# Keys and values of a memory: computed in the opening of the program, with their weights loaded in turn with those of a modulation

## The chip, the cores and the metric

One NeuronCore of a Trainium2 chip runs the whole program. The metric is the time of one execution on the device, in microseconds (us); shown is the median of repeated runs. PE is TensorE, DVE is VectorE, ACT is ScalarE, POOL is GpSimd, and SP is the queue that issues most DMA loads.

## What is computed

Two models stand one after the other. The first has two hybrid layers over 512 latent and 256 context tokens of width 1024. Each layer normalizes and modulates the tokens, with shift, scale and gate from silu(c) @ w_mod, multiplies by w_in (3584 columns), and mixes by a short convolution, an attention, a gated scan (hgrn) and a Fourier mix, then multiplies by w_out. The second model has one layer: a window attention and a gated delta rule side by side, a cross attention to a memory of 256 rows, and a swiglu. What the change moves is the memory's part of that cross attention; in the reference's terms:

```
m  = rms_norm(mem, g_mem)              # 256 x 1024
kv = m @ w_ckv                         # 1024 x 2048: 1024 columns of keys, 1024 of values
```

It depends on nothing of the first model. The first modulation, on which all of layer 0 depends, is

```
shift, scale, gate = split(silu(c) @ w_mod + b_mod, 3)    # w_mod: 1024 x 3072 per layer
```

## The kernel before, in words

Every large product runs in float32 precision as three matmuls (`mm3`, lines 189 to 191): each operand is split into a high part (an ACT copy, line 194) and a low part (a subtraction, line 195, on DVE or, where `pool_lo` is set, on POOL). Weights come in units of 1 MB (`wraw`, line 279, two buffers `raw`), are split into tiles `wh` and `wl` of 128 x 512 (four buffers of each, which is one unit), and the split of the next unit follows PE through those buffers, one unit ahead. A unit of 256 columns against 256 columns of tokens is 48 matmuls of 128 x 256.

The program builds instructions in the order of the Python code, by generators that several places advance in turn, and a scheduler then orders each engine's queue; what stands in a queue runs in that order.

**Start** (`start`, `mod_first`, lines 330 to 362, and `start_ctx`). The context rows are loaded, scaled by their root mean square (`rowscale`, lines 416 to 418) and transposed (line 532). The shift and scale columns of w_mod for layer 0 come in eight tiles `mraw` of 1 MB, one for each k, and four matmuls `modA` for each accumulate the modulation in PSUM (line 346). Then the first weight unit of layer 0 and the rows of x are loaded. At the end modA is copied, transposed (line 318) and made into A and B (`mod_ab`), the context is rescaled with them (line 512, tile `xc`) and split, and the first layer matmuls (`gc` for context columns, `gl` for latent ones) begin. The gate rows of the modulation come later, in steps between the layers' matmuls; the first of these matmuls is line 380.

**The memory** (`memkv`, lines 673 to 720) is a generator of nine steps. The first loads and scales the 256 rows and transposes them into `mch` and `mcl`, high and low part (lines 428, 445, 446). Four steps make the keys, two groups of 24 matmuls each, and four the values, likewise. A result leaves PSUM by an ACT copy into a tile `t` of two buffers (lines 705, 718) and goes to DRAM by a DMA on ACT's queue (lines 706, 719). Its units of w_ckv are split one ahead.

It runs in three places. The first step stands in the attention of layer 1 (line 1042). The keys follow that attention in `layer` (lines 560 to 563); in PE's queue they fill the attention's last part. The values are made at the beginning of `part2` (lines 1184 to 1190), that is, after the output projection of layer 1 (`out_proj`, tile `wo`), whose last rows are meanwhile normalized and transposed (`to_xT`) for part 2.

**Attention of layer 1.** For a token tile and a head PE makes scores (lines 1058, 1059), DVE the maximum (line 1063), ACT the exponential (line 1066), DVE the scaling (line 1068), PE six transposes (line 1074), ACT and DVE copy them, and PE multiplies with the values (line 1083).

**Part 2** begins in `mix` with a product for values, alpha and beta (144 columns, token tiles 0 to 3 in turn, lines 1306 to 1318), then a group of 128 columns (`dn_proj`). Beside them run `rope2`, which loads the positions by ACT's queue (line 1440) and makes sines on DVE and ACT (lines 1443 to 1460), and `dn_gates`, a chain of small DVE operations from alpha to the gates, whose first matmul is line 1566.

Of the kernel before, what the change touches and what calls it, by code (L numbers as in the profile page):

```python
# [9 lines left out]
F32 = mybir.dt.float32  # L10
# [12 lines left out]
T = S + CTX  # L23
# [4 lines left out]
def constants():  # L28
# [54 lines left out]
    # window masks [query, key]: block before (key >= query), block after (key <= query)  # L83
# [6 lines left out]
class Cols:  # L90
    """a [128, T] operand in two tiles: latent columns and context columns"""
# [9 lines left out]
def pair(t, pr):  # L101
    """the columns of two token tiles of t [128, 512]"""
    if pr[1] == pr[0] + 1:
        return t[:, 128 * pr[0]:128 * pr[0] + 256]
    return t[:, 0:S].rearrange("p (a c) -> p a c", c=128)[:, pr[0]:pr[1] + 1:pr[1] - pr[0]]


class Ahead:
    """split weight units in the order of their use, one ahead"""
# [14 lines left out]
class PhasePool:  # L124
    """sets K.ps_s for a phase"""
# [12 lines left out]
class Slots:  # L138
    """tiles in given places, by tag"""
# [8 lines left out]
class K:  # L148
    order = ((0, 1), (2, 3))
    # rows of w_out in the order in which they get ready: hgrn, fourier, conv, attention  # L150
# [46 lines left out]
    def load_early(self):  # L197
        """identity, parameters as columns, silu of the conditions"""
# [10 lines left out]
        # silu(c), silu(c_ctx) as 32 column operands, two used  # L209
# [5 lines left out]
    def lower_bounds(self):  # L215
        nc, cst = self.nc, self.cst
        # hgrn lower bounds: logits in col 32..39 as (d, l, j)
# [9 lines left out]
        # per (d, j): bias lb + floor, scale 1 - lb  # L227
# [8 lines left out]
    def load_late(self, tp):  # L236
        """constants of part 2"""
# [17 lines left out]
        # a_log, dt_bias, sink on every partition  # L255
# [3 lines left out]
    def rpow(self, out, ss, scale, eps, n):  # L259
        """out = (ss * scale + eps) ** -0.5 on small [128, n]"""  # L260
# [5 lines left out]
    def wraw(self, srcs, kk, cols):  # L266
        """raw tile [128, kk, cols]; srcs: list of (col0, dram ap [kk*128, n])"""
# [14 lines left out]
    def wsplit(self, raw_view, tiles=None):  # L282
        """[128, kk, ...] -> list of (hi, lo) [128, cols] over k, at most 512 columns in a tile; tiles: others than the usual"""
# [21 lines left out]
    def mod_rows(self, t, l, c0, n):  # L305
        """bias rows of w_mod columns c0.. in t [32 n + stream, 512], the rest zero"""
# [6 lines left out]
    def mod_ab(self, l, mr):  # L313
        """A = g (1 + scale), B = shift as [128, stream, 8] of mr rows (shift 0, 1, scale 0, 1)"""
# [15 lines left out]
    def mod_first(self, mp, side):  # L330
        """shift and scale of layer 0"""
# [3 lines left out]
        next(side)  # L335
        def load(k):
            raw = mp.tile([128, 2048], F32, tag="mraw", name="mraw", bufs=5)
            nc.sync.dma_start(raw, self.I["w_mod"][0, 128 * k:128 * k + 128, 0:2048])
            return raw

        raws = [load(k) for k in range(5)]
        for k in range(8):
            raw = raws[k]
            next(side, None)
            for n in range(4):
                nc.tensor.matmul(pa[32 * n:32 * n + 32], self.cact[:, k, :], raw[:, 512 * n:512 * n + 512],
                                 start=(k == 0), stop=(k == 7))
            if k < 3:
                raws.append(load(k + 5))
            if k == 2:  # L350
                self.pool_lo = True
                self.first = self.hgrn_w(self.I["w_in"][0], 0)
                self.pool_lo = False
                self.xrows = []
                for i in range(4):
                    h = mp.tile([128, 1024], F32, tag="h", name="h", bufs=6)
                    nc.sync.dma_start(h, self.I["x"][0, 128 * i:128 * i + 128, :])
                    self.xrows.append(h)
        for _ in side:
            pass  # L360
# [3 lines left out]
    def mod_rest(self):  # L364
        """gate rows of both layers to DRAM, shift and scale of layer 1: a step per MB of weights"""
# [3 lines left out]
        def gates(l):  # L369
            # rows 64 q + 32 n + stream: columns 512 n of the k tiles of parity q  # L370
# [40 lines left out]
    def rowscale(self, h, pool):  # L411
        """h [128, 1024] -> h / rms(h) rows, in place"""
# [8 lines left out]
    def to_xT(self, xs, pr, xh, xl, A, B, pool):  # L421
        """xs: row-scaled token tiles of the pair pr; their columns of xh/xl[k]"""
# [25 lines left out]
    def lat_gemm(self, us, tags):  # L448
        """psum [128 ch, 512] per unit; first all units on the first 256 tokens"""
# [1613 lines left out]
```

## Time and profile before

| | |
|---|---|
| median of 3 runs | 1797.39 us |
| lowest, highest | 1796.39, 1798.08 us |
| span of the profiled execution | 1802.5 us |
| busy: PE, PE weight loads, DVE, ACT, POOL | 94%, 75%, 56%, 50%, 13% of the span |
| mean granted TensorE clock | 0.974 |
| DMA, all loads and stores | 193.79 MB, mean 108 GB/s |

The profile gives the span of one execution, the time from its first to its last instruction; the timed runs are others, so both are named. Busy shares are means over stages with different limits. Matmuls overlap, so a PE that is busy all the time may still follow its operands; the distance between the starts of two matmuls says more than their lengths.

### The profile page before, as it was taken

What the parts mean: (1) busy time and instruction counts of PE and PEld (TensorE: products, weight loads), DVE (VectorE), ACT (ScalarE), POOL (GpSimd) and SP (SyncE); (2) the same over time, 40 slices, a digit from 0 to 9 for tenths busy, and PEclk for the clock granted to TensorE, in tenths of its full rate; (3) what the DMA queues carried; (4) which work ended last, traced back from release to release, by engine and by line L of the source; (5) the groups of instructions that cost most, each with busy time, mean ns of one, the idle gap of its engine ahead of it and who ended that gap; (6) DMA issues with size and microseconds to landing.
All of it is one profiled execution on the core that took longest, in us unless ns stands there. A gap on an engine that the chain in (4) does not pass through costs nothing.

```text
span 1802.5 us, 30443 instructions
## 1 busy us (share of the span) xinstructions
PE 1693.4 (94%) x12155; PEld 1357.9 (75%) x12155; DVE 1017.6 (56%) x2127; ACT 902.7 (50%) x1850; POOL 232.4 (13%) x250
## 2 busy tenths in 40 slices
PE   6999889999989988999999888999999999999998
PEld 3876767878768665877878667877788788888886
DVE  4446373565474646476576898568766733333233
ACT  4756562442458765353565833465655633333222
POOL 2100001101131000100022434002000111111000
PEclk8999999999999999999999998899999999999999
DMA  8231203200454211301764233110743723332531
GB/s 351 106 115 49 94 25 133 88 1 26 147 183 143 95 48 38 111 24 53 251 213 143 87 90 94 42 48 1 215 136 107 248 79 94 94 94 84 174 105 70
DMA packets 162570, 193.79 MB, mean 108 GB/s; under 512 B 15054, under 2 KB 124910, under 8 KB 160252
## 3 DMA queue, kind: packets, MB, share of 16 engines
q1 hardware_dynamic: 156604, 183.37, 31.3%
q10 hardware_dynamic: 5824, 8.47, 1.6%
q8 instruction: 95, 1.56, 0.4%
q14 instruction: 47, 0.39, 0.1%
HBM read 175.28 MB, written 13.66 MB: 105 GB/s over the span
## 4 chain that ended last, share of the span: by engine, by line
PE 69%; DVE 13%; ACT 8%; issue 4%; DMA 2%; POOL 2%; ACTq 0%; SPq 0%; POOLq 0%; DVEq 0%
PE mm L189 7%; PE mm L190 7%; PE mm L191 7%; PE gl L189 4%; PE gl L190 4%; PE gl L191 4%; DVE acc L1603 2%; PE tr L1083 2%; DVE wl L195 2%; PE sc L1059 1%; PE tr L1074 1%; PE sc L946 1%; ACT S L860 1%; PE tp L189 1%; PE tp L190 1%
## 5 line engine op out<-in xcount | busy, mean ns | idle before, releaser
L194 ACT ACTIVATE wh<-raw 128x512 fp32r<-128x512 f32 (+1 forms) x458 | 282.6, 628 | 409.0 <-PE mm L190 161.0
L195 DVE TENSOR_TENSOR wl<-raw,wh 128x512 fp32r<-128x512 f32 x416 | 285.1, 699 | 358.2 <-ACT wh L194 350.4
L189 PE MATMUL mm<-xh,wh 128*128 128x512 f32 x520 | 208.3, 401 | 1.4 <-ACT acc L1601 1.0
L190 PE MATMUL mm<-xl,wh 128*128 128x512 f32 x520 | 208.3, 401 | 0.0
L191 PE MATMUL mm<-xh,wl 128*128 128x512 f32 x520 | 208.1, 401 | 0.0
L189 PE MATMUL gl<-xh,wh 128*128 128x512 f32 (+1 forms) x480 | 181.3, 378 | 1.3 <-ACT lf L754 0.6
L191 PE MATMUL gl<-xh,wl 128*128 128x512 f32 (+1 forms) x480 | 180.1, 376 | 0.3 <-DVE wl L195 0.3
L190 PE MATMUL gl<-xl,wh 128*128 128x512 f32 (+1 forms) x480 | 179.7, 375 | 0.1
L189 PEld LDWEIGHTS mm<-xh,wh 128*128 128x128 f32 x520 | 100.6, 193 | 23.2 <-ACT acc L1601 1.9
L191 PEld LDWEIGHTS mm<-xh,wl 128*128 128x128 f32 x520 | 100.3, 193 | 20.4
L190 PEld LDWEIGHTS mm<-xl,wh 128*128 128x128 f32 x520 | 100.3, 193 | 20.2 <-issue 0.3
L189 PEld LDWEIGHTS gl<-xh,wh 128*128 128x128 f32 x480 | 91.7, 191 | 23.0 <-issue 6.0
L191 PEld LDWEIGHTS gl<-xh,wl 128*128 128x128 f32 x480 | 91.7, 191 | 19.0 <-issue 4.9
L190 PEld LDWEIGHTS gl<-xl,wh 128*128 128x128 f32 x480 | 91.8, 191 | 15.5 <-issue 2.8
L195 POOL TENSOR_TENSOR wl<-raw,wh 128x512 fp32r<-128x512 f32 x42 | 59.6, 1425 | 108.0 <-ACT wh L194 73.5
L189 PE MATMUL gc<-ch,wh 128*128 128x256 f32 x224 | 65.7, 295 | 4.1 <-ACT ch L194 2.7
L190 PE MATMUL wo<-wl,yh 128*128 128x512 f32 x160 | 65.1, 408 | 4.2 <-DVE wl L195 4.2
L190 PE MATMUL gc<-cl,wh 128*128 128x256 f32 x224 | 65.2, 291 | 1.8 <-DVE cl L195 1.8
L191 PE MATMUL gc<-ch,wl 128*128 128x256 f32 x224 | 65.1, 291 | 0.0
L191 PE MATMUL wo<-wh,yl 128*128 128x512 f32 x160 | 63.6, 399 | 0.0
L189 PE MATMUL wo<-wh,yh 128*128 128x512 f32 x160 | 63.4, 402 | 0.0
L1979 POOL TENSOR_TENSOR al<-t,ah 128x512 fp32r<-128x512 f32 x22 | 28.3, 1286 | 211.6 <-ACT ah L1978 211.6
(596 smaller groups left out, 3926.4 us busy)
## 6 DMA issues: line engine op xcount, KB each, us to landing
raw<-in_w_in SPq DMA_DIRECT2D x32, 1024.0 KB, 4.9
raw<-in_w_gate_up SPq DMA_DIRECT2D x44, 512.0 KB, 4.8
raw<-in_w_mod SPq DMA_DIRECT2D x16, 1024.0 KB, 6.3
raw<-in_w_out SPq DMA_DIRECT2D x12, 1024.0 KB, 5.3
raw<-in_w_down SPq DMA_DIRECT2D x10, 1024.0 KB, 4.9
mraw<-in_w_mod SPq DMA_DIRECT2D x8, 1024.0 KB, 12.0
raw<-in_w_out SPq DMA_DIRECT2D x16, 512.0 KB, 6.5
raw<-in_w_ckv SPq DMA_DIRECT2D x8, 1024.0 KB, 5.0
```

The costliest lines, as they stand in the source:

```text
L189: mm(out, ah, bh, start=start, stop=False)
L190: mm(out, ah, bl, start=False, stop=False)
L191: mm(out, al, bh, start=False, stop=stop)
L194: self.nc.scalar.activation(hi, src, AF.Copy)
L195: (eng or self.nc.vector).tensor_tensor(lo, src, hi.bitcast(F32), ALU.subtract)
L860: nc.scalar.activation(so.rearrange("p v c -> p c v"), up, AF.Copy)
L946: nc.tensor.matmul(o[32 * A:32 * A + 32, p, 64 * i:64 * i + 64], *t[n_], start=(n_ == 0), stop=(n_ == len(t) - 1))
L1059: nc.tensor.matmul(s_[:, c0:c0 + n], qi[hs], kl[hs, ks], start=False, stop=True)
L1074: nc.tensor.transpose(tr[:, 128 * ii:128 * ii + 128], P[:, 128 * (t0 + ii):128 * (t0 + ii) + 128], self.ident)
L1083: nc.tensor.matmul(o[64 * h:64 * h + 64], kv[:, k0 + kt, 128 + 64 * h:192 + 64 * h], PTs[h][:, 128 * kt:128 * kt + 128], start=(kt == 0), ...
L1603: nc.vector.scalar_tensor_tensor(acc, pad[:, t:t + 512], cw, acc, ALU.mult, ALU.add)
L1979: nc.gpsimd.tensor_tensor(al[j], t, ah[j].bitcast(F32), ALU.subtract)
```

## The change

`mod_first` now begins with the memory. It makes the generator `memkv`, takes its first step, and then takes one step of it for each of the eight k of w_mod: a unit of keys or values, then a load of a later w_mod tile, then a step of the context's transposes (from k = 2 on), then the four modA matmuls of k. Two w_mod tiles are asked for ahead of the loop, with four buffers in place of five. The first weight unit of layer 0 is loaded and split after the loop, its low parts no longer on POOL, and the rows of x are asked for at k = 6. `memkv` loads its first weight unit before it scales the rows, and uses tiles of the start's pool. The three old places are gone. (The edit also drops comments and docstrings, which changes line numbers: a line here can be 1 to 4 off from the old one.)

```diff
     def mod_first(self, mp, side):
         pa = self.psum("sm", [128, 512], "modA")
         mr = mp.tile([128, 512], F32, tag="mr", name="mr")
-        next(side)
         def load(k):
-            raw = mp.tile([128, 2048], F32, tag="mraw", name="mraw", bufs=5)
+            raw = mp.tile([128, 2048], F32, tag="mraw", name="mraw", bufs=4)
             nc.sync.dma_start(raw, self.I["w_mod"][0, 128 * k:128 * k + 128, 0:2048])
             return raw
-        raws = [load(k) for k in range(5)]
+        self.mkp = mp
+        mem = self.memkv(mp)
+        next(mem)
+        raws = [load(k) for k in range(2)]
+        self.xrows = []
         for k in range(8):
-            raw = raws[k]
-            next(side, None)
+            next(mem)
+            if k < 6:
+                raws.append(load(k + 2))
+            if k >= 2:
+                next(side, None)
             for n in range(4):
-                nc.tensor.matmul(pa[32 * n:32 * n + 32], self.cact[:, k, :], raw[:, 512 * n:512 * n + 512],
+                nc.tensor.matmul(pa[32 * n:32 * n + 32], self.cact[:, k, :], raws[k][:, 512 * n:512 * n + 512],
                                  start=(k == 0), stop=(k == 7))
-            if k < 3:
-                raws.append(load(k + 5))
-            if k == 2:
-                self.pool_lo = True
-                self.first = self.hgrn_w(self.I["w_in"][0], 0)
-                self.pool_lo = False
-                self.xrows = []
+            if k == 6:
                 for i in range(4):
                     h = mp.tile([128, 1024], F32, tag="h", name="h", bufs=6)
                     nc.sync.dma_start(h, self.I["x"][0, 128 * i:128 * i + 128, :])
                     self.xrows.append(h)
+        for _ in mem:
+            pass
+        self.first = self.hgrn_w(self.I["w_in"][0], 0)
         for _ in side:
             pass
...
     def layer(self, l):
-                if l:
-                    self.mkp = ap
-                    for _ in range(4):
-                        next(self.mem)
...
     def memkv(self, mk):
         for i in range(2):
-            h = mk.tile([128, 1024], F32, tag="mem", name="mem", bufs=2)
+            h = mk.tile([128, 1024], F32, tag="h", name="mem", bufs=6)
             nc.sync.dma_start(h, I["mem_2"][0, 128 * i:128 * i + 128, :])
+            xs.append(h)
+        w = I["w_ckv_2"][0]
+        units = Ahead(...)
+        units.more()
+        for h in xs:
...
         self.to_xT(xs, (0, 1), mh, ml, self.col[:, c0:c0 + 8], None, mk)
         yield
-        w = I["w_ckv_2"][0]
-        units = Ahead(...)
...
     def attention(self, l, w_in, need, ap):
-        if l:
-            self.mem = self.memkv(ap)
-            next(self.mem)
...
     def part2(self):
-            self.mkp = mk
-            for _ in self.mem:
-                pass
```

SP's queue at the very beginning of the program; `mem` is the memory, `mraw` w_mod, `h` context or x, `raw` a weight unit. Before:

```order
L524 DMA h<-in_ctx 128x1024 x2
L338 DMA mraw<-in_w_mod 128x2048 x8
L279 DMA raw<-in_w_in 128x8x128 x2
L357 DMA h<-in_x 128x1024 x4
L497 DMA k_blockones<-in_c_blockones 128x128
```

and with the change:

```order
L681 DMA mem<-in_mem 128x1024 x2
L279 DMA raw<-in_w_ckv 128x8x256
L337 DMA mraw<-in_w_mod 128x2048 x2
...
L528 DMA h<-in_ctx 128x1024 x2
L337 DMA mraw<-in_w_mod 128x2048
L279 DMA raw<-in_w_ckv 128x8x256 x2
...
L358 DMA h<-in_x 128x1024 x4
L279 DMA raw<-in_w_in 128x8x128 x2
L501 DMA k_blockones<-in_c_blockones 128x128
```

The eight w_mod tiles stood together behind the context; now the memory stands first, units of w_ckv and tiles of w_mod take turns, the context comes after five of them, and x and the first unit of w_in after all.

PE's queue at the end of the attention of layer 1; `sc` are scores, `tr<-early,P` transposes, `tr<-PT,kv` products with the values, `mm<-mch,wh` the memory's keys, `wo` the output projection. Before:

```order
L1074 MATMUL tr<-early,P 128x128 x6
L189 MATMUL mm<-mch,wh 128x256
L190 MATMUL mm<-mcl,wh 128x256
L191 MATMUL mm<-mch,wl 128x256
...
L1083 MATMUL tr<-PT,kv 64x128 x12
L189 MATMUL mm<-mch,wh 128x256
...
L191 MATMUL mm<-mch,wl 128x256
L189 MATMUL wo<-wh,yh 128x512
```

and with the change:

```order
L1073 MATMUL tr<-early,P 128x128 x6
L1057 MATMUL sc<-kh,qs 128x512
L1058 MATMUL sc<-kl,qs 128x512
L1057 MATMUL sc<-kh,qs 128x256
L1058 MATMUL sc<-kl,qs 128x256
L1073 MATMUL tr<-early,P 128x128 x6
L1082 MATMUL tr<-PT,kv 64x128 x12
L1073 MATMUL tr<-early,P 128x128 x12
L1082 MATMUL tr<-PT,kv 64x128 x12
L189 MATMUL wo<-wh,yh 128x512
```

Before, 57 of the memory's matmuls stood between these rows and 135 between the last product with the values and the projection's first matmul; now 18 matmuls of the projection stand ahead of the last two heads' scores, and its 19th comes right behind the last product.

ACT's queue where part 2 begins; `xh` are high parts of the transposed rows, `pos` the positions, `rp` the sines, `V` the evacuation of part 2's first product, `vd<-t` the store of memory values, `wh` split weights. Before:

```order
L445 ACTIVATE xh<-tr,col 128x256 x2
L719 DMA vd<-t 128x256
L1562 ACTIVATE al<-bc 128x8
L1440 DMA pos<-in_positions 128x1024
L718 ACTIVATE t<-mm 128x256
...
L1456 ACT_TABLE_LOAD
L1456 ACTIVATE rp_10221<-ra,k_invf 128x512
L1460 ACTIVATE rp_10221<-ra 128x512
L1317 ACTIVATE V<-mm 128x128 x3
L194 ACTIVATE wh<-raw 128x512 x4
```

and with the change:

```order
L449 ACTIVATE xh<-tr,col 128x256 x8
L1313 ACTIVATE V<-mm 128x128
L1558 ACTIVATE al<-bc 128x8
L1436 DMA pos<-in_positions 128x1024
L1313 ACTIVATE V<-mm 128x128 x2
L194 ACTIVATE wh<-raw 128x512
L1452 ACT_TABLE_LOAD
L1452 ACTIVATE rp_10221<-ra,k_invf 128x512
L194 ACTIVATE wh<-raw 128x512 x3
L1313 ACTIVATE V<-mm 128x128
```

Before, the sines were made ahead of the first evacuation `V`, while the memory's values ran; now the positions' load stands behind the first of them, and the sines between the third and the fourth, ahead of three weight splits.

## Rows read from the trace of the kernel before

**Rows 1.** The page, costliest groups: engine, operation, tiles, count, busy us, mean ns.

```profile
L195 DVE TENSOR_TENSOR wl<-raw,wh 128x512 fp32r<-128x512 f32 x416 | 285.1, 699 | 358.2 <-ACT wh L194 350.4
```

**Rows 2.** Busy us of each engine by stretch, then granted clock, DMA share, GB/s.

```profile
0.00:10.00 10.00, 1.76 (x3) 0.37 (x3) 2.40 (x15) 5.07 (x8) 1.54 (x7) 1.00 0.82 316
...
10.00:20.00 10.00, 9.16 (x53) 3.01 (x54) 2.82 (x7) 1.53 (x4) 0.55 (x1) 1.00 1.01 425
...
30.00:40.00 10.00, 5.54 (x25) 5.24 (x26) 9.24 (x21) 6.19 (x14) 6.03 (x7) 0.51 1.05 407
```

**Rows 3.** Timeline of PE in the start: start us, length, operation, count, idle before.

```profile
10.53 0.47 PE L532 MATMUL mm<-early,h 128*128 128x128 f32 x1
...
12.25 1.93 PE L346 MATMUL modA<-mraw,cact 128*32 128x512 f32 x6
...
16.77 0.38 PE L532 MATMUL mm<-early,h 128*128 128x128 f32 x2
...
16.99 0.38 PE L532 MATMUL tr<-early,h 128*128 128x128 f32 x2
...
17.82 2.78 PE L346 MATMUL modA<-mraw,cact 128*32 128x512 f32 x24
...
26.08 1.93 PE L346 MATMUL modA<-mraw,cact 128*32 128x512 f32 x8 [1.41 <-DMA mraw<-in_w_mod]
...
32.69 0.80 PE L189 MATMUL gc<-ch,wh 128*128 128x256 f32 x2 [2.70 <-ACT ch L194]
```

**Rows 4.** Timeline of DVE and POOL in the start.

```profile
11.03 0.76 DVE L418 TENSOR_SCALAR h<-h,st 128x1024 f32<-128x1024 f32 x1 [0.67 <-POOL st L263]
...
28.33 4.99 POOL L195 TENSOR_TENSOR wl<-raw,wh 128x512 fp32r<-128x512 f32 x4 [17.33 <-ACT wh L194]
...
30.89 3.98 DVE L512 TENSOR_SCALAR xc<-xc,A,B 128x256 f32<-128x256 f32 x5
```

**Rows 5.** One source line, L380: ns min/median/max, first and last start.

```profile
L380 PE MATMUL sm<-raw,cact x32: 592/605/617, 60.9 to 97.4; 128*32 128x512 f32 x32
```

**Rows 6.** The tile mcl, low part of the transposed memory, on DVE.

```profile
L446 DVE SCALAR_TENSOR_TENSOR mcl<-tr,col,mch x8: 473/478/485, 772.4 to 779.7; 128x256 fp32r<-128x256 f32 x8
```

**Rows 7.** Timeline at the end of the attention of layer 1.

```profile
839.22 0.95 DVE L1063 TENSOR_REDUCE ast<-sc 128x1 f32<-128x768 f32 x1
...
842.54 0.97 ACT L1066 ACTIVATE P<-sc,ast,rq 128x768 f32<-128x768 f32 x1
...
855.50 2.46 PE L1083 MATMUL tr<-PT,kv 128*64 128x128 f32 x24
...
858.11 0.28 PE L190 MATMUL mm<-mcl,wh 128*128 128x256 f32 x1
...
858.23 0.28 PE L191 MATMUL mm<-mch,wl 128*128 128x256 f32 x1
```

**Rows 8.** The tile wo: output projection of layer 1, one of its three lines.

```profile
L189 PE MATMUL wo<-wh,yh x64: 388/392/496, 874.2 to 924.6; 128*128 128x512 f32 x64
```

**Rows 9.** Timeline from the end of that projection into part 2.

```profile
924.60 0.39 PE L189 MATMUL wo<-wh,yh 128*128 128x512 f32 x1
...
925.06 0.40 PE L191 MATMUL wo<-wh,yl 128*128 128x512 f32 x1
...
934.47 0.75 DVE L662 TENSOR_SCALAR xs<-hn,ss 128x1024 f32<-128x1024 f32 x1 [0.44 <-POOL pad L1591]
...
943.30 0.42 ACTq L1440 DMA_DIRECT2D pos<-in_positions  x1
...
947.62 0.43 DVE L1443 CAST ra<-pos 128x512 f32<-128x512 int32 x1 [0.54 <-DMA pos<-in_positions]
...
965.96 0.18 DVE L1318 COPY ab<-mm 128x16 f32<-128x16 f32 x1
```

**Rows 10.** Timeline of PE at the gates' first matmul.

```profile
979.16 1.04 PE L1566 MATMUL sm<-dg,k_tri 128*128 128x16 f32 x4 [3.18 <-DVE dg L1563]
```

**Rows 11.** Timeline of ACT: an evacuation of the memory's values.

```profile
938.06 0.38 ACT L718 ACTIVATE t<-mm 128x256 f32<-128x256 f32 x1 [1.57 <-DMA vd<-t]
```

More of the change, by code (lines that the diff above doesn't have):

```diff
@@ L679, in memkv @@
         for i in range(2):
-            h = mk.tile([128, 1024], F32, tag="mem", name="mem", bufs=2)
+            h = mk.tile([128, 1024], F32, tag="h", name="mem", bufs=6)
             nc.sync.dma_start(h, I["mem_2"][0, 128 * i:128 * i + 128, :])
-            st = mk.tile([128, 4], F32, tag="ast", name="mst", bufs=4)
+            xs.append(h)
+        w = I["w_ckv_2"][0]
+        units = Ahead([lambda c=c: self.unit_cp([(0, w[:, c:c + 256])]) for c in range(0, 1024, 256)]
+                      + [lambda c=c: self.wsplit(self.wraw([(0, w[:, c:c + 256])], 8, 256)) for c in range(1024, 2048, 256)])
+        units.more()
+        for h in xs:
+            st = mk.tile([128, 4], F32, tag="mst", name="mst", bufs=2)
             for j in range(2):
-                junk = mk.tile([128, 512], F32, tag="fd", name="junk", bufs=2)
+                junk = mk.tile([128, 1024], F32, tag="junk", name="junk", bufs=1)[:, :512]
                 nc.scalar.activation(junk, h[:, 512 * j:512 * j + 512], AF.Square, accum_out=st[:, j:j + 1])
@@ L688, in memkv @@
             nc.vector.tensor_scalar(h, h, st[:, 3:4], None, ALU.mult)
-            xs.append(h)
         self.to_xT(xs, (0, 1), mh, ml, self.col[:, c0:c0 + 8], None, mk)
@@ L693, in memkv @@
         self.vd = self.dr.tile([128, 2, 1024], F32, tag="vd", name="vd")
-        w = I["w_ckv_2"][0]
-        units = Ahead([lambda c=c: self.unit_cp([(0, w[:, c:c + 256])]) for c in range(0, 1024, 256)]
-                      + [lambda c=c: self.wsplit(self.wraw([(0, w[:, c:c + 256])], 8, 256)) for c in range(1024, 2048, 256)])
         for j2 in range(4):
```

## The prediction

> **What bounds the kernel now.** I first read the page: the table of engines, then the split rows. TensorE (PE) is busy nearly everywhere, and one split of a weight tile into its low part costs VectorE (DVE) 0.70 us [rows 1]. So time is PE's matmuls plus the stretches in which PE has nothing to do, and the change matters as far as it moves PE work into such stretches or opens new ones. I then read busy time by stretch [rows 2]: in the first 40 us PE is short of work, while the DMA engines are full and move about 400 to 425 GB/s. There the reader sees a start that waits for 8 MB of w_mod. The timeline of that start [rows 3] shows the last modA matmuls ending at 26.08 + 1.93 = 28.0 and the first layer matmul at 32.69. After that I looked for the places that the memory's matmuls leave: the end of the attention of layer 1 [rows 7] and the step into part 2 [rows 9]. In both the memory's matmuls run back to back, 0.12 us apart (858.11 to 858.23) [rows 7], and everything that ends a stage hides behind them.
>
> PE's order in the changed kernel equals the old one from the middle of the first layer's first matmuls to the scores of layer 1, and again from the third token tile of part 2's first matmul on. So the sum has one term in the start and three in the middle.
>
> **Term 1, the start: later by 40.0 us.** I compare at the first gate-row matmul (L380), at 60.9 now [rows 5].
> - The memory's rows are now normalized where the context's were. The second of those row scalings ends at 11.03 + 0.76 = 11.8 [rows 4]; the squares now come in halves, so I take 12.2.
> - DVE's order then has four weight splits, 4 x 0.70 = 2.8 [rows 1], up to 15.0, and the eight low parts of the transposed memory. They take 0.48 each alone and were spread over 772.4 to 780.2 in the old place, about 1.0 each [rows 6]. Here they go in turn with transposes through two PSUM buffers; I take 0.6 (nearer to the first, since little else is queued): 4.8, up to 19.8. By PE's order, 22 of the 384 memory matmuls are done by then.
> - From there PE has 362 x 0.12 = 43.4 [rows 7], seven k steps of modA at 2.78 / 3 = 0.93 (24 records are three steps) = 6.5, and 16 context transposes of at most 0.38 / 2 = 0.19, 3.0 together [rows 3]: 52.9, up to 72.7. The splits (per unit of 48 matmuls, 5.8 us of PE, DVE has 2.8) and the loads fit beside it: up to the last w_mod tile there are 17 MB, 17.8 / 0.425 = 42 us at the rate of rows 2. With a little for the seams, modA ends at 73.0.
> - From modA's end to L380 it takes 60.9 - 28.0 = 32.9 now. Three things shorten it: the five rescalings that took 3.98 while POOL split the first weights beside them [rows 4] no longer have that neighbour (up to 2.0); the four row scalings of x, 0.76 each [rows 4], are done earlier (I count half, 1.5); part of the stretch at a granted clock of 0.51, near the lower level of 1.2 GHz [rows 2], may be spared since PE comes from dense work (1.5). That leaves 27.9. It can't be below PE's own work there, 144 matmuls at 0.12, 36 transposes at 0.11 (two by every 0.22, rows 3) and some 4 us of first gap: 25.3. The upper bound is 32.9.
> - 73.0 + 27.9 = 100.9, so +40.0; with the bounds, +35 to +47.
>
> At the opening a rule bears on this. The granted clock reads 1.00 in the first 20 us [rows 2], but the records disagree: one transpose took 0.47 at 10.53, and from 16.77 two went by every 0.22; six modA records took 1.93 at 12.25, and 24 took 2.78 at 17.82 [rows 3]. I add nothing for it, since up to 19.8 DVE sets the pace; if PE ran on at the lower level as long as from 32.69 to 40 [rows 2, 3], half of 7.3 us, 3.6, would be added, which the upper bound holds. The Trainium skill (TensorE: Matmul & The Clock Gate, What's actually happening) says that the throttled state is the default and activity releases it. By it the sum would be some 2 to 4 us higher; the durations agree with it, the clock column doesn't.
>
> **Term 2, the transposes of the memory: earlier by 2.0 us.** Sixteen leave the attention of layer 1, where PE is full: 0.11 to 0.19 each [rows 3], 1.8 to 3.0; I take 2.0.
>
> **Term 3, the end of the attention: earlier by 19.0 us.** 192 matmuls leave, 23.0 us. Of these 57 (6.8 us) stood between the last scores and covered the softmax chain (maximum 0.95, exponential 0.97, then scaling, transposes and 2.46 of matmuls [rows 7]); PE's new order has 18 matmuls of the output projection there, 4.2 us. So the chain, not PE, ends this stage, and the last of the 2.46 stays near 855.50 + 2.46 = 858.0. The projection's 19th matmul then waits for the last product and one split, about 1.3: 859.3. Now it comes at 874.2 + 18 x 0.23 = 878.3 [rows 8] (two of these in 0.46, 924.60 to 925.06 [rows 9]). Bounds: 23.0 if nothing opens, 15 if the chain slips by 4.
>
> **Term 4, into part 2: earlier by 12.4 us.** Another 192 matmuls, 23.0, leave the stretch from the projection's end (925.46) to the gates' first matmul (979.16) [rows 9, 10], 53.7. They hid two chains.
> - The last rows are scaled at 935.2, 9.8 after the end [rows 9]; with fewer splits in DVE's queue I take 9.2. Eight transposed tiles with high and low part follow, at about 0.68 through two PSUM buffers: 14.6. PE has only 48 small matmuls to put beside that.
> - ACT's order now issues the load of the positions after all eight high parts and the first evacuation: 15.2. It took 947.62 - 943.30 = 4.3 to land [rows 9], with less traffic I take 3.7: 18.9. DVE waits for it, in order, ahead of the rotation's nine operations (five of 0.43, four like a split, 0.70: 5.0) and of the next weights' splits: 24.
> - Another 4 us of splits and rotation stand before the last evacuation: 28.1. From there to the gates' first matmul it is 979.16 - 965.96 = 13.2 [rows 9, 10], a chain of small DVE operations for which PE waits already now, 3.18 us. So 41.3, and 53.7 - 41.3 = 12.4 saved. Upper bound 21.8 if the positions hold up nothing, lower 9.
>
> **Sum.** +40.0 - 2.0 - 19.0 - 12.4 = +6.6. The profiled execution's span is 1802.5, 0.3% above the median of the timed runs, 1797.4; I put the difference on the median: **1804.0 us**.
>
> **The rivals.** *A: faster.* The memory's matmuls fill the DMA-bound start and leave the middle at nearly their full price. For it: PE is idle for much of the first 40 us [rows 2]. Against: it can't begin before about 12, and the middle loses its cover. If the start's tail takes 25.3 (-2.6), the low parts 0.48 each (-1.0), the attention gives 22 (-3.0), and the positions land before the transposes end, so that part 2 gives 19 (-6.6), the sum is 6.6 - 13.2 = -6.6: 1790.8. It is decided in part 2: with the other terms as above the change gains once the gates' first matmul comes less than 53.7 - 19.0 = 34.7 us after the projection's end. The Trainium skill (Perfetto Trace Analysis, Optimization Strategy) says for a kernel with several regimes that interleaving them may help; that is this rival.
>
> *B: slower still.* The memory's results go through two buffers and leave by DMA from ACT's queue, now while the loads fill the DMA engines. ACT's evacuation waits when a store needs more than two groups of 24 matmuls less the copy, 2 x 2.88 - 0.38 = 5.4 us, and the weight splits queue behind it on ACT, then PE. One such wait is in the trace, 1.57 us [rows 11]. Against: the loads in the start leave pauses, since PE takes 6.7 us for each 2 MB. Seven waits of 1.57 add 11: 1815.0.
>
> **How the numbers follow.** No change means within 0.2%, 3.6 us, about what the timed runs can tell. The forecast has 58%: its own range is 1798 to 1811, so 41 slower, 16 within, 1 faster. Rival A has 30%: 21 faster and 9 within. Rival B has 12%, all slower. That gives 0.22, 0.25 and 0.53. The range from 1791 to 1815 reaches to both rivals and takes in the bounds of the terms except all of them together.
>
> **What would show it.** In the changed profile: modA's last record near 73, the first gate-row matmul near 101, PE dense from about 20 to 72; the last attention matmuls without memory matmuls between, and 1 to 4 us of idle PE there; after the projection's last matmul an idle PE of 10 us or more in two pieces, released by DVE, with the positions' load and the rotation before the second; the gates' first matmul about 41 after the projection's end. It is wrong if modA ends before 69 or after 78, if ACT waits for stores of the keys or values, or if the stretch into part 2 takes less than 35.

## The result and the profile after

The changed kernel takes 1819.16 us (median of 4 runs, 1812.7 to 1822.92) where the kernel before takes 1796.89 (4 runs, 1795.98 to 1798.08): a ratio of 1.0108, 95% interval 1.0073 to 1.0143. The medians lie 22 us apart, and by the interval of the ratio the loss is 13 to 26 us. The same kernel timed again, in experiment 11, gives 1.0101 (1.0079 to 1.0124). The forecast was 1804.0 with a range from 1791 to 1815: slower, as forecast, but by 22 between the medians in place of 6.6, and outside the range.

Five places in PE's order cut the program; four of them bound the terms of the sum, and the end of layer 0's projection parts what lies ahead of the old places from what lies in them. "Again" is the profile of the second timing of the same kernel, "forecast" is the prediction's sum laid on the times of before.

| us | before | forecast | after | again |
|---|---|---|---|---|
| last modA matmul starts | 27.0 | | 79.0 | 79.0 |
| first gate-row matmul | 60.9 | 100.9 | 108.8 | 108.7 |
| last matmul of the output projection of layer 0 | 534.2 | 574.2 | 579.9 | 580.2 |
| last matmul of the output projection of layer 1 | 925.1 | 944.1 | 955.8 | 948.0 |
| gates' first matmul | 979.2 | 985.8 | 998.9 | 991.9 |
| span of the profiled execution | 1802.5 | 1809.1 | 1820.7 | 1814.4 |

The start grew by 47.9 us where 40.0 were forecast; the way from the gate rows to the end of the projection shrank by 17.2 (again: 24.9) where 21.0 were, 15.0 (23.1) of it behind layer 0's projection, where the memory's matmuls are gone; the way into part 2 by 11.0 (10.2) where 12.4 were. What lies behind the gates' first matmul takes 821.8 (822.5), before 823.3.

The single lines of the changed kernel by source, with first and last start, answer to [rows 5] and [rows 10] (x96 is layer 0's part of the x160):

```profile
L353 PE MATMUL modA<-mraw,cact x64: 592/605/1062, 14.2 to 79.0; 128*32 128x512 f32 x64
L384 PE MATMUL sm<-raw,cact x64: 592/605/617, 108.8 to 630.8; 128*32 128x512 f32 x64
L191 PE MATMUL wo<-wh,yl x96: 389/397/478, 491.4 to 579.9; 128*128 128x512 f32 x96
L191 PE MATMUL wo<-wh,yl x160: 387/397/628, 491.4 to 955.8; 128*128 128x512 f32 x160
L1562 PE MATMUL sm<-dg,k_tri x4: 262/263/283, 998.9 to 999.2; 128*128 128x16 f32 x4
```

PE's busy time by stretch in the changed kernel answers to [rows 2] (columns: stretch, length, busy us and records, granted clock, DMA share, GB/s):

```profile
20.00:40.00 20.00, 20.00 (x164) 1.00 0.89 325
40.00:50.00 10.00, 9.39 (x67) 1.00 0.92 336
60.00:70.00 10.00, 9.13 (x71) 1.00 0.99 366
```

The reader sees a start that PE now bounds: it is busy for 9.1 to 10 of every 10 us from 20 to 80, and the DMA engines are no longer full throughout. The idle time of [rows 2] was used, but 46 us of matmuls (384 x 0.12) were put where the three stretches of [rows 2] had 13.5 us free, and the one that they leave out, here from the kernel before, another 4.3:

```profile
20.00:30.00 10.00, 5.75 (x36) 0.81 1.05 397
```

The timeline of PE in the changed kernel's start, answering to [rows 3], shows what made it longer than forecast (start, length, operation, count of records, idle before and its releaser):

```profile
16.07 0.69 PE L432 MATMUL tr<-early,mem 128*128 128x128 f32 x2
17.64 0.28 PE L191 MATMUL mm<-mch,wl 128*128 128x256 f32 x1
17.76 0.28 PE L189 MATMUL mm<-mch,wh 128*128 128x256 f32 x1
...
29.80 1.06 PE L353 MATMUL modA<-mraw,cact 128*32 128x512 f32 x8
30.79 0.38 PE L189 MATMUL mm<-mch,wh 128*128 128x256 f32 x1
...
43.79 1.04 PE L353 MATMUL modA<-mraw,cact 128*32 128x512 f32 x2
44.77 0.33 PE L536 MATMUL mm<-early,h 128*128 128x128 f32 x1
45.02 1.06 PE L353 MATMUL modA<-mraw,cact 128*32 128x512 f32 x6
...
49.94 0.50 PE L189 MATMUL mm<-wh,mch 128*128 128x256 f32 x2 [0.35 <-ACT wh L194]
...
62.34 1.04 PE L353 MATMUL modA<-mraw,cact 128*32 128x512 f32 x2
64.26 0.39 PE L189 MATMUL mm<-wh,mch 128*128 128x256 f32 x1 [0.87 <-ACT t L720]
...
70.20 1.06 PE L353 MATMUL modA<-mraw,cact 128*32 128x512 f32 x6
71.19 0.38 PE L189 MATMUL mm<-wh,mch 128*128 128x256 f32 x1
...
72.21 1.04 PE L353 MATMUL modA<-mraw,cact 128*32 128x512 f32 x2
73.19 0.38 PE L190 MATMUL mm<-wl,mch 128*128 128x256 f32 x1
...
78.51 1.06 PE L353 MATMUL modA<-mraw,cact 128*32 128x512 f32 x6
```

A modA group is four matmuls (eight records, two for each) into four parts of one PSUM tile. A whole one holds PE from 29.80 to 30.79, 0.99 us. Of three groups the changed queue pulled the first matmul off (43.79 from 45.02, 62.34 from 70.20, 72.21 from 78.51): alone it holds PE from 72.21 to 73.19, 0.98 us, and three together hold it from 70.20 to 71.19, as long. Standing together the four overlap, and a group in two pieces is paid twice.

### The profile page after: what moved, and what is told of

It is laid out like the page before. It is cut to its first block, busy times and chain, and to the rows that moved or that the text cites. A ratio compares the mean times of both kernels' runs of the same rounds, so it can differ in the third digit from the quotient of the medians.

```text
span 1820.7 us, 30451 instructions
## 1 busy us (share of the span) xinstructions
PE 1705.3 (94%) x12155; PEld 1367.3 (75%) x12155; DVE 1017.9 (56%) x2131; ACT 911.3 (50%) x1856; POOL 226.0 (12%) x246
## 5 line engine op out<-in xcount | busy, mean ns | idle before, releaser
L195 DVE TENSOR_TENSOR wl<-raw,wh 128x512 fp32r<-128x512 f32 (+1 forms) x420 | 287.2, 698 | 378.6 <-ACT wh L194 375.9
L190 PEld LDWEIGHTS mm<-xl,wh 128*128 128x128 f32 x520 | 100.2, 193 | 20.4
L195 POOL TENSOR_TENSOR wl<-raw,wh 128x512 fp32r<-128x512 f32 x38 | 55.1, 1456 | 79.2 <-ACT wh L194 55.8
```

The source lines that it names most:

```text
L190: mm(out, ah, bl, start=False, stop=False)
L195: (eng or self.nc.vector).tensor_tensor(lo, src, hi.bitcast(F32), ALU.subtract)
```

## The experiments

Each run has its expectation as it stood before it ran. Every ratio is to the kernel before on the same chip.

**1. The memory left out** (`memkv` replaced by stores of a constant tile):

```diff
     def memkv(self, mk):
+        t = mk.tile([128, 256], F32, tag="mt", name="t", bufs=1)
+        nc.gpsimd.memset(t, 0.5)
+        yield
+        for j in range(8):
+            nc.scalar.dma_start(self.kd[:, j, :], t)
+            nc.scalar.dma_start(self.vd[:, j // 4, 256 * (j % 4):256 * (j % 4) + 256], t)
+            yield
```

> Leaves out the memory's keys and values: a constant tile is stored in their place, so the cross attention works on constants. Theory (in the start the memory's matmuls cost their full time and more, in the middle about half of it): first gate-row matmul at 61 to 66 instead of 108.8, the middle as in the changed kernel (43 us from the projection's end to the gates' first matmul), time 1819 - 46 = 1773 us, so the memory costs 24 in its old places and 46 in its new one. Rival (the loss lies in the granted clock or in later stages, and the old places charged the full 46 us of matmuls): 1797 - 46 = 1751 us.

Measured: 0.9895 (0.9864 to 0.9927), that is 1778 on the scale of 1797; first gate-row matmul 72.9, last projection matmul 913.3, gates' first matmul 956.1. The middle is 23.8 us shorter up to the projection's end and 11.3 into part 2: in its old places the memory cost some 35 us, of 46 us of matmuls and some 2 of transposes, where the expectation had 24. The rival (1751) falls. The start was a miss: 72.9 where 61 to 66 were expected, with no memory in it. The 2 MB of stores of the constant stand among the loads there, so the run doesn't tell what the new order alone costs; run 6 does, as far as it can be had without the memory.

**2 and 3. One half back.** In run 2 the keys stay in the start and the values return to part 2, in run 3 the other way round; either time the rows are scaled and transposed once more in the attention of layer 1 (`memkv_old` is the old generator with one of its two loops):

```diff
+        if l:
+            self.mem = self.memkv_old(ap)
+            next(self.mem)
         other = self.fourier(l, w_in, need, tabs, ap)
...
             self.load_late(mk)
+            self.mkp = mk
+            for _ in self.mem:
+                pass
```

> Keys stay in the start, values return to part 2 (their memory rows are scaled and transposed in the attention of layer 1 again). Theory: first gate-row matmul 26 us earlier than in the changed kernel, at 83 (22.9 of matmuls, 2 of modA groups that are no longer pulled apart, 1 of seams); the way from the projection's end to the gates' first matmul 54 again instead of 43, 2 us for the transposes: 1819 - 26 + 11 + 2 = 1806 us. Rival (a fixed price for putting the memory's rows, scaling and transposes first, whatever number of matmuls follows): first gate-row matmul still after 95, time 1819 or more.

> Values stay in the start, keys return to the attention of layer 1, with their own scaling and transposes there. Theory: first gate-row matmul at 83; the end of the attention 15 us longer again and 2 us for the transposes: 1819 - 26 + 17 = 1810 us. Rival (a fixed price for the memory's rows first): first gate-row matmul after 95, time 1825 or more.

Measured: values back 1.0057 (1.0039 to 1.0075), keys back 1.0103 (1.0074 to 1.0133). The gate-row lines of both:

```profile
L384 PE MATMUL sm<-raw,cact x64: 589/592/617, 88.0 to 608.2; 128*32 128x512 f32 x64
```

```profile
L384 PE MATMUL sm<-raw,cact x64: 592/605/617, 89.4 to 612.0; 128*32 128x512 f32 x64
```

So the start's price goes with the matmuls: half of them cost 27.1 and 28.5 us, all of them 47.9, and the fixed price of the rival (after 95) falls. Run 2's time is as expected, run 3's some 5 us over its 1810.

What the middle gave back differs. With the keys gone from it, the way from the gate rows to the projection's end is 23.0 shorter, but 3.9 of that lie ahead of the end of layer 0's projection, where no work was moved. The lines of the kernel before, then of run 2:

```profile
L191 PE MATMUL wo<-wh,yl x96: 390/397/478, 445.6 to 534.2; 128*128 128x512 f32 x96
L191 PE MATMUL wo<-wh,yl x160: 387/397/497, 445.6 to 925.1; 128*128 128x512 f32 x160
```

```profile
L191 PE MATMUL wo<-wh,yl x96: 389/397/478, 468.9 to 557.4; 128*128 128x512 f32 x96
L191 PE MATMUL wo<-wh,yl x160: 387/397/504, 468.9 to 929.2; 128*128 128x512 f32 x160
```

From one projection's end to the next it is 371.8 for 390.9, 19.1 shorter. Runs 5, 10 and 12, which also have the keys alone in the start, give 15.9, 18.6 and 18.2, and run 3, with the keys in their old place, gives 1.4. So the keys gave back 16 to 19 of their 23.0 us of matmuls. With the values gone (run 3), the way into part 2 is 44.0 long in place of 54.1: 10.1 of 23.0. A half costs more than half of 47.9, since the stretch from modA's end to the gate rows is 35.8 and 35.7 (modA's last matmul starts at 51.6 and 53.1, lasting 0.6) where the changed kernel has 29.2. In SP's queue of the run with the values back, and from SP's waits between 26 and 50 (total, times, longest):

```profile
34.77 11.70 SPq L337 DMA_DIRECT2D mraw<-in_w_mod  x3
46.52 2.20 SPq L358 DMA_DIRECT2D h<-in_x  x4
48.81 3.72 SPq L279 DMA_DIRECT2D raw<-in_w_in  x2
...
SPq L337 <- DMA kd<-t: 11.2, 3, 6.8
```

The last w_mod tiles take SP 11.70 us to issue, and x and the first unit of layer 0 stand behind them. Of what these tiles wait for, there and just ahead, 11.2 us are stores of keys (`kd<-t`) and 6.5 us matmuls of PE, so the four buffers are not the whole of it. With keys and values in the start these come in time, because PE is busy until 79 anyway.

**4. The positions earlier** (the DMA moved from ACT's queue to SP's, at the beginning of `mix`):

```diff
+            nc.sync.dma_start(pi_.rearrange("p s t -> p (s t)"), p32.to_broadcast([128, 2 * S]))
             raw = self.wraw([(0, w[:, 640:768]), (128, w[:, 2816:2832])], 8, 144)
...
-        nc.scalar.dma_start(pi_.rearrange("p s t -> p (s t)"), p32.to_broadcast([128, 2 * S]))
```

> The changed kernel with the positions' load issued by SP at the beginning of part 2's mixing, ahead of its first weights, in place of ACT's queue behind the transposed rows. Theory: VectorE no longer waits 2.3 us for it in order, the way from the projection's end to the gates' first matmul is 40 to 41 instead of 43, time 1816 us. Rival (the transposes of the last rows alone set that stretch, the positions are hidden): 43 as before, 1819 us.

Measured: 1.0108 (1.0074 to 1.0142), and 42.9 from the projection's end (952.9) to the gates' first matmul (995.8): the rival's number. In the changed kernel DVE waited for the load, here it doesn't and begins the rotation at once. First the changed kernel, then this run:

```profile
976.18 0.43 DVE L1439 CAST ra<-pos 128x512 f32<-128x512 int32 x1 [2.32 <-DMA pos<-in_positions]
```

```profile
970.58 0.26 DVE L1318 COPY ab<-mm 128x16 f32<-128x16 f32 x2
970.81 0.42 DVE L1440 CAST ra<-pos 128x512 f32<-128x512 int32 x1
...
976.24 0.28 ACT L1317 ACTIVATE V<-mm 128x128 f32<-128x128 f32 x1 [5.67 <-PE mm L191]
```

ACT then waits 5.67 us for PE, which runs the third token tile at the lower level. Granted clock of the stretch, the changed kernel first, then this run:

```profile
970.00:980.00 10.00, 8.72 (x64) 0.84 0.16 52
```

```profile
970.00:980.00 10.00, 9.37 (x44) 0.50 0.00 0
```

That doesn't mean that the lower clock came in the wait's place. The second profile of the changed kernel (run 11) has the lower clock and the wait together, by its stretch and by its timeline:

```profile
963.00:973.00 10.00, 9.37 (x44) 0.50 0.15 52
```

```profile
968.60 0.43 DVE L1439 CAST ra<-pos 128x512 f32<-128x512 int32 x1 [2.57 <-DMA pos<-in_positions]
971.36 0.28 ACT L1313 ACTIVATE V<-mm 128x128 f32<-128x128 f32 x1 [5.67 <-PE mm L191]
```

That profile takes 43.9 to the gates' first matmul, so beside the profile with the same clock the wait of 2.57 us was worth 1.0; run 3, with 0.50 and a wait of 2.34, takes 44.0. The clock of this stretch varies from execution to execution, and the first profile, with 0.84, hides that 1.0.

**5. x and the first unit earlier**, keys alone in the start:

```diff
         for k in range(8):
             next(mem, None)
+            if k == 3:
+                self.pool_lo = True
+                self.first = self.hgrn_w(self.I["w_in"][0], 0)
+                self.pool_lo = False
+            if k == 2:
+                for i in range(4):
+                    h = mp.tile([128, 1024], F32, tag="h", name="h", bufs=6)
+                    nc.sync.dma_start(h, self.I["x"][0, 128 * i:128 * i + 128, :])
```

> As the run with the values returned to part 2 (keys alone in the start, 1.0057 of the time before), but with the rows of x and the first weight unit of layer 0 asked for ahead of the last four w_mod tiles, and that unit's low parts on GpSimd. Theory (SP's queue stands still on w_mod tiles that wait for their four buffers, x and the first unit behind them come late, so that 35.8 us pass from the last modA matmul to the first gate-row matmul instead of 28.9 in the changed kernel): 29 to 30 us there, first gate-row matmul at 82 instead of 88, time 6 us less, ratio 1.002 to the kernel before. Rival (that stretch is set by the rescaling of the context and the lower clock): 35 to 36, 88, ratio 1.0057.

Measured: 1.0047 (1.0028 to 1.0066). From modA's end (57.0 + 0.6) to the gate rows (85.3) it is 27.7 in place of 35.8, a little under the expected 29 to 30, so the late loads did set that stretch. But modA ended 5.4 later, behind those loads, and only 2.7 was left at the gate rows. The time isn't clear of run 2's: half a hit.

**6. The start's order alone**, on the kernel before, with the memory in its old places:

```diff
-            raw = mp.tile([128, 2048], F32, tag="mraw", name="mraw", bufs=5)
+            raw = mp.tile([128, 2048], F32, tag="mraw", name="mraw", bufs=4)
...
-        raws = [load(k) for k in range(5)]
+        raws = [load(k) for k in range(2)]
...
+        self.first = self.hgrn_w(self.I["w_in"][0], 0)
         for _ in side:
             pass
```

> The kernel before with only the start's order of the change: four w_mod buffers, two tiles asked for ahead, x at the seventh k, the first weight unit of layer 0 after the loop and not on GpSimd; the memory stays in its old places. Theory (part of the start's price has nothing to do with the memory's matmuls): first gate-row matmul at 66 to 73 instead of 60.9, time 5 to 12 us over the kernel before. Rival (the order costs nothing without the memory's matmuls): 61, ratio 1.000.

Measured: 1.0023 (1.0004 to 1.0042); first gate-row matmul at 64.2, 3.3 later than before, under the expected 5 to 12. The order has a price, but a small one. It lies behind modA, whose last matmul starts at 26.8 (27.0 before): PE waits 8.3 us there for the rows of x, which are loaded later and are scaled by DVE.

**7 and 9. Whole modA groups.** In run 7 a section that the scheduler may not split holds each group; in run 9 the groups of the last two k are queued behind the memory step ahead of them, and the context's step stands behind the group:

```diff
+            with self.tc.issue_after(self.last.ins) if k >= 6 else ExitStack():
                 for n in range(4):
                     nc.tensor.matmul(pa[32 * n:32 * n + 32], self.cact[:, k, :], raws[k][:, 512 * n:512 * n + 512],
```

> The changed kernel with each group of four modA matmuls kept together in TensorE's queue (by a section that the scheduler may not split, which adds branches). Theory (a group that is pulled apart costs its 0.98 us twice, three are): the last modA matmul ends at 77 instead of 79.9, less what the branches cost. Rival (the groups are not what made the start longer than forecast): 80 or later.

> The changed kernel with its modA groups whole, without branches: the groups of the last two k are queued behind the memory step ahead of them, and the context's transposes of a step behind its group. Theory (three groups that were pulled apart cost 0.98 us each once more): the last modA matmul ends at 77.0 instead of 79.9, first gate-row matmul at 106, time 3 us less than the changed kernel, ratio 1.009 to 1.010. Rival (the lost time is in waits for weights and stores): modA ends at 79.5 or later, ratio 1.011.

Run 7 was inconclusive: 1839.8 in a single execution, its last modA matmul at 90.7. PE stands for 21.8 us ahead of the eight groups in which it waits for nothing that the profile shows, and that hides what the groups give. Run 9 measured 1.0063 (1.0038 to 1.0089). Its timeline of PE shows the group that stood in two pieces at 43.79 and 45.02, now whole, and the wait for t:

```profile
44.11 1.07 PE L352 MATMUL modA<-mraw,cact 128*32 128x512 f32 x8
45.11 0.44 PE L537 MATMUL mm<-early,h 128*128 128x128 f32 x2
...
63.99 0.38 PE L189 MATMUL mm<-wh,mch 128*128 128x256 f32 x1 [1.95 <-ACT t L721]
```

The last modA matmul starts at 77.5 (79.0), the gate rows at 106.6 (108.8): 1.5 and 2.2 earlier, less than the 2.9 and 2.8 expected and between theory and rival, while the wait for t grew from 0.87 to 1.95: the pulled-off matmul at 62.34 had stood in front of it. 1.5 + 1.1 = 2.6 is close to 3 x 0.98. Its time lies 7 to 8 us under the changed kernel's, more than 2.2 us explain, with intervals of 4 us on either side. The two profiles are 14.4 apart (1820.7 and 1806.3): 2.2 are the start's, but 2.8 lie between the gate rows and the end of layer 0's projection and 6.2 behind the gates' first matmul, where both kernels queue the same work. So most of the difference between these two profiles isn't the groups'.

**8. Four buffers for t:**

```diff
-                t = self.mkp.tile([128, 256], F32, tag="mt", name="t", bufs=2)
+                t = self.mkp.tile([128, 256], F32, tag="mt", name="t", bufs=4)
```

> The changed kernel with four buffers for the tile t through which keys and values leave, in place of two. Theory (the stores hold TensorE up by one wait of 0.87 us in all): the last modA matmul ends at 79, the time is the same within 2 us. Rival B of the prediction (evacuations wait for stores): modA ends before 75 and the time falls by 5 or more.

A single execution: 1820.0 us, modA's last matmul starts at 78.3 (79.0), the gate rows at 108.5. In the changed kernel ACT does wait for stores, 3.8 us for one of keys and 3.5 for one of values, as rival B of the prediction has it; here these waits are gone. Rival B falls by its price: the stores hold PE for under 1 us in all.

**10 and 12. A version to beat both.** Keys alone in the start, a modA group behind each half unit, x ahead of the last w_mod tiles; run 12 also has eight buffers of h:

```diff
-            yield
+                yield
...
-            h = mk.tile([128, 1024], F32, tag="h", name="mem", bufs=6)
+            h = mk.tile([128, 1024], F32, tag="h", name="mem", bufs=8)
```

> Keys alone in the start (values in part 2), one modA group behind each half unit of 24 matmuls, the rows of x and the first weight unit ahead of the last w_mod tiles. Theory (the groups free their buffers early, so SP's queue no longer stands, and TensorE's own work sets the start): last modA matmul at 51 to 53 as without the earlier x (52.2), then 28 us as with it, first gate-row matmul at 80 to 81 in place of 85.3 and 88.0, ratio 1.001 to 1.002. Rival (the 17 MB of loads set the end of modA): it ends at 57 or later, ratio 1.005. That the memory's place is free, and the kernel is faster than before: below 0.998.

> As the run with the keys alone in the start and one modA group behind each half unit, but with eight buffers for rows (tile h) in place of six, so that the rows of x need not wait for those of the memory. Theory (SP stood 10.84 us on two rows of x that waited for a buffer, and ACT's squares of x held up the split of the last key unit): last modA matmul ends at 52 to 56 instead of 64.8, then 26 to 28 us, first gate-row matmul at 79 to 83 in place of 91.2, ratio 1.000 to 1.002. Rival (the loads as a whole set the end of modA): 60 or later, ratio 1.004.

Measured: 1.0049 (1.0032 to 1.0067) and 1.0060 (1.0038 to 1.0082); gate rows at 91.2 and 89.0. Both missed: modA ends at 64.8 and 62.1, which is what their rivals gave as the sign that the loads set it. The x rows hold SP as long with eight buffers as with six; run 10 first, then run 12, each with what SP waited for (total, times, longest):

```profile
27.81 10.84 SPq L355 DMA_DIRECT2D h<-in_x  x4
...
SPq L355 <- DMA kd<-t: 9.2, 2, 5.2
```

```profile
26.52 10.92 SPq L355 DMA_DIRECT2D h<-in_x  x4
...
SPq L355 <- DMA kd<-t: 9.1, 2, 6.3
```

So a buffer of h isn't what SP stood on. The profile names stores of keys: two rows of x are issued only when such a store has landed. Why a load has to wait for a store these views don't tell, and no run tried it. In run 12 PE waits for the last key unit's split (1.74 and 1.39 us), which stands behind the squares of x in ACT's queue, and modA ends at 62. No version tried is faster than the kernel before.

**11. The changed kernel once more.**

> The changed kernel itself once more, for its stretches beside those of the runs above. Theory (the start's price is fixed by the order of the queues, the end of the attention varies with the granted clock): first gate-row matmul at 108 to 109 again, last output-projection matmul at 947 to 956, ratio 1.010 to 1.012. Rival (the start itself varies from run to run): first gate-row matmul over 1 us away from 108.8.

Measured: 1.0101 (1.0079 to 1.0124). The start is the same within 0.1 (108.7), but the projection ends at 948.0, 7.8 earlier than in the first profile. The end of the attention, first profile and then this one:

```profile
899.83 0.85 PE L1073 MATMUL tr<-early,P 128*128 128x128 f32 x6 [1.18 <-DVE P L1067]
...
901.21 4.09 PE L1082 MATMUL tr<-PT,kv 128*64 128x128 f32 x24 [0.53 <-ACT PT L1077]
905.23 0.50 PE L189 MATMUL wo<-wh,yh 128*128 128x512 f32 x1
```

```profile
897.33 0.85 PE L1073 MATMUL tr<-early,P 128*128 128x128 f32 x6 [1.18 <-DVE P L1067]
...
898.71 2.45 PE L1082 MATMUL tr<-PT,kv 128*64 128x128 f32 x24 [0.53 <-ACT PT L1077]
901.09 0.50 PE L189 MATMUL wo<-wh,yh 128*128 128x512 f32 x1
```

Granted clock and busy time of PE over these rows, in the same order:

```profile
899.80:905.20 5.40, 4.84 (x30) 0.68 0.00 0
```

```profile
897.30:901.10 3.80, 3.24 (x31) 1.00 0.00 0
```

The waits are the same to the hundredth; the 24 products take 4.09 us where the stretch has a granted clock of 0.68 and 2.45 where it has 1.00. Run 9 shows the slow form too (4.10), runs 4 and 8 the fast one. That is 1.6 of the 7.8 us. Another 3.7 come in the projection behind it (50.6 us from its 19th matmul to its last, for 46.9), where the first profile has two waits for weight splits, 1.30 and 1.24 us, that the second hasn't; the rest lies ahead of these rows. From the end of layer 0's projection to that of layer 1's, the first profile and runs 4, 7, 8, 9 and 11, which leave the attention alone, are 15.0, 19.0, 19.4, 20.4, 19.1 and 23.1 shorter than before.

## Why the prediction was wrong, point by point

- **What bounds the kernel: right.** The start's idle PE was used up, the two chains of the middle lost some of their cover. The direction follows.
- **Term 1 failed: 47.9 for 40.0, above its bound of 47.** The step is "seven k steps of modA at 0.93" with "a little for the seams", up to 73.0. What comes of these seven steps holds PE for 9.8 us in place of 6.5, and the last modA matmul ends at 79.0 + 0.6 = 79.6, past the 78 that the prediction named as a sign of being wrong. Of the 6.6 missing, 2.9 are three groups pulled apart (3 x 0.98); run 9 got 1.5 of them back, since the wait for t grew by 1.1. The order of the changed kernel, which I had, lists one modA matmul, then other work, then three; I counted records and not pieces. Another 1.7 are waits of PE for t, for the first split of the values and for a copy of the context (0.87 + 0.35 + 0.23 + 0.26). The last 2.0 is what is left over; part of it stands at the changes between kinds of matmul, none of it was tried by itself, and its cause stays open. The bounds moved only the way behind modA (25.3 to 32.9 gives +37.4 to +45.0) and had some 2 us for all of PE's 53. The rest of the term held: from modA's end to the gate rows 29.2 for 27.9.
- **The lower clock at the opening: nothing to add, as taken.** Transposes still took 0.69 at 16.07, but from 17.64 the memory's matmuls go 0.12 apart, ahead of the 19.8 from which PE set the pace. The Trainium skill (TensorE: Matmul & The Clock Gate, What's actually happening) says that activity releases the throttled state; these rows agree, and the 2 to 4 us that it would have added don't appear.
- **Terms 2 and 3: right in size, with a spread that I hadn't priced.** 21.0 forecast, 15.0 and 23.1 behind layer 0's projection in two executions of one program. For the keys alone, 19.0 was forecast and 16 to 19 came. The 1 to 4 us of idle PE at the softmax chain are there (1.18 + 0.53 and, in the heads ahead of it, 0.57), and in some executions the clock is lower behind them.
- **Term 4: right, one step of it wrong.** 11.0 and 10.2 for 12.4, the gates' first matmul 43.1 and 43.9 after the projection's last matmul starts, for 41.7 (41.3 from its end). The step that names the positions' load as what DVE waits for is right as a row (2.32 and 2.57 us) and too high as a price: run 4 took the wait away and gained 1.0 beside the profile with the same clock. That PE's clock would be lower there (0.50 over ten us in run 11) stood in no term.
- **Rival A, free work in an idle start,** had its point in part 2 (34.7 us; it took 43). The start wasn't idle enough: runs 2 and 3 show 27.1 and 28.5 us for 23 us of matmuls each. The Trainium skill (Perfetto Trace Analysis, Optimization Strategy) says that interleaving the regimes of a kernel that has several may help; here it lost, since one of the two regimes had less room than the work moved, and the other needed that work as cover.
- **From the profiles to the times.** At the gates' first matmul the changed kernel is 19.7 and 12.7 behind, and 6.6 were forecast. The medians differ by 22 and 16, the spans by 18.2 and 11.9. A time is 1.8 us longer than its span (1822.51 for 1820.7), so the one profiled execution of the kernel before took some 1804 us, 5 to 7 above its medians, and the profiles show less of the loss than the times do. Two stretches in which all versions queue the same matmuls are long in that execution: from the gate rows to the end of layer 0's projection it takes 473.3, the thirteen other profiles 465.9 to 474.3, 471.2 in the mean, and from the gates' first matmul to the end 823.3, the others 815.6 to 823.9, 820.9 in the mean. That is 4.5 of the 5 to 7; why they were long stays open.

## What to carry to other kernels

Before work is moved into a stretch in which an engine is idle, work out when that engine becomes the bound there: beyond that point every us moved costs a us, while the place that it left gives back only what it had not been covering. Here the keys had covered a short chain and came back by 16 to 19 of 23.0, the values had covered a long one and came back by less than half (10.1). Before a gain of one version is read from two profiles, look at the stretches that it leaves alone: here each of the two that every version queues alike differs by 8 us over fourteen profiles. Look in the new queue for groups that only pay as a group, and count pieces, not instructions.

## What the runs showed of the hardware

- A modA matmul of 32 columns by 512 holds PE for 0.98 us alone, and four of them into four parts of a tile for 0.99 together (29.80 to 30.79), as long as no other matmul stands between them.
- One program, same waits: 24 products in 2.45 us at a granted clock of 1.00 or in 4.09 at 0.68, both behind 1.7 us of idle PE. An uncovered chain costs its idle time and, in some executions, the clock behind it.
- A load can stand in SP's queue until a store from ACT's queue has landed, and every load behind it with it: 9.2 of 10.84 us for four rows of x in run 10, 9.1 of 10.92 in run 12; more buffers for x didn't change that.
